# Head units by ScalarE a unit ahead, mix transfers on GpSimd's queue, an up tile moved before w_o, and a tail summed by TensorE, in a one-layer streaming encoder

## The chip, the cores and the metric

One core of one Trainium2 chip runs the whole program. The time is the device time of one execution in microseconds (us). The engines are TensorE (PE, matmuls), VectorE (DVE), ScalarE (ACT), GpSimd (POOL) and SyncE (SP, which here only issues DMA transfers). Each engine runs its own instructions in order and waits on semaphores for the others. A DMA is issued by an engine's instruction stream; here SP issues most, GpSimd and ScalarE a few.

## The reference, cut to what matters

1024 prompt frames and 32 sample frames of width 1024 go through one layer: an adaLN-modulated input gemm whose columns feed three head groups, one output gemm, a layer norm, a gated feed-forward part, and a second layer norm.

```python
h = x * (1 + sc1) + sh1
mq, mk, mv, mo, mi, mf, fq, fk, fv, ff, gu, gv = split(h @ w_in)
hm = head_norm(mlstm(mq, mk, mv, mi, mf)) * norm_g * sigmoid(mo)    # 4 heads of 64
hf = fox(fq, fk, fv, log_sigmoid(ff))                               # 8 heads of 64, causal softmax
hg = spatial_gate(gu, layer_norm(gv))                               # 4 groups of 64
mix = concat([hm, hf, hg]) @ w_o
x = layer_norm(ALPHA * x + (1 + g1) * mix)
h = x * (1 + sc2) + sh2
y = (silu(h @ w_gate) * (h @ w_up)) @ w_down
x = layer_norm(ALPHA * x + (1 + g2) * y)
```

Besides x, the keys and values of the heads, the mLSTM states and the gate inputs are outputs.

## The kernel before

**Arithmetic.** All data are fp32. Each operand of a large gemm is split into a part `hi` in a reduced format (float32r) and the rest `lo`, and a product is three matmuls, hi·hi, hi·lo and lo·hi (`gemm`, L117 to L119). Weights are loaded, `hi` is cast by ScalarE (L105) and `lo` is a subtraction on VectorE, or on GpSimd where a unit asks for that (L106). Activations are split in the same way (L922 and L923 for the mix that w_o reads). fp32 matmuls that are not split do transposes, the small products of the mixers, and the column sums of the layer norms (`ln_means`, L876, against a matrix of 1/1024).

**Layout.** Tokens lie in the free dimension, in two groups: group 0 has 512 prompt frames, group 1 the other 512 and the 32 sample frames. Features lie in 128-partition tiles. Intermediate head data (q, k as `dqh`, `dql`; mLSTM's `dmqk`, `dmv`, `dmo`; the gate input `dvn`; the mix `dmix`) go through DRAM: they are stored by one unit and loaded by another. `load` (L87) and `store` (L91) issue on SP's queue.

**Stages.** First adaLN and the gemm of the value units; then the gates; then a list ORDER of units: `q0` to `q7` are the gemms of q and k of one fox head (`fm_unit` with `evac_qk`), `k0`, `k1`, `o`, `v` the mLSTM projections, `s` its states, `f0` to `f7` the fox heads of group 0, `m0` to `m3` mLSTM tiles of 128 tokens, `a` pieces of the adaLN gemm. A `p` behind a unit gives its weight splits to GpSimd. Then come the gMLP gates (`evac_gv`, `evac_gmlp`, `to_mix`), w_o of group 0 with its norm, the remaining q units, and then the mixers of group 1 (fox heads in two parts, mLSTM tiles 4 to 8) woven into the up and down products of the feed-forward part of group 0. Before the last of these groups of up tiles (`g == WOB`) stands w_o of group 1, whose norm is woven into the up tiles left (`fill`). Then up, a variant of up with fewer products (`sup`), and down of group 1 follow, in two halves at the end, and the last layer norm (`ln2`).

**What sets the order.** The program is written as a sequence of units; a scheduler with a cost model then orders the instructions of each engine, with raised priority for the f and m units of ORDER, and with some instructions tied behind another (`issue_after`). Buffers are rings of a fixed count per name, so a new use of a name waits for the last reader of the buffer it gets.

**The places of the change.**
- `evac_qk` (L358 on) takes a finished q/k product out of PSUM: ScalarE writes `hi` (L366), VectorE writes `lo` from PSUM (L371), GpSimd adds them for `kr` (L372), and three stores follow.
- `mlstm` loads six pieces per tile: mqk, two for mqb, mv, mo, mb. ScalarE makes three passes over mo (L542 to L544), and GpSimd multiplies it by the norm's weight (L545).
- `to_mix` transposes a finished tile on TensorE, copies it out on ScalarE (L637, buffer `mixs`, of which there are two) and stores it to `dmix`. mLSTM calls it with k0 = 0, gMLP with k0 = 6.
- A fox head ends with a copy on ScalarE into `fo` (L762), an addition on VectorE into `fr` (L763) and a store to `dmix`. `foxbufs` are the buffer counts of a fox head's k1, qp, k2 and others; `fox_qp` is the name of the loaded queries (read by L706).
- `ln_sum` adds the z tiles of a layer norm on GpSimd and their squares on VectorE (L866), as each down tile is finished (L963). `ln_means` sums over the partitions. In `ln2` the mean is copied out (L1206), the variance is formed (L1207), each tile has its mean subtracted (L1209), is multiplied by 1/std (L1225), and gets its weight and bias from ScalarE (L1227) or, the last one, from VectorE (L1229).

Of the kernel before, what the change touches and what calls it, by code (L numbers as in the profile page):

```python
# [7 lines left out]
F32 = mybir.dt.float32  # L8
# [7 lines left out]
P = 128  # L16
D = 1024
KT = 8
# [23 lines left out]
ORDER = "q0 f0 q1 a f1 a q2 f2 k0 k1p s a q3 f3 a v q4 f4 a q5 f5 o a m0 q6 f6 a m1 a q7 m2 f7 a m3 a"  # L42
# [23 lines left out]
def f(ap):  # L66
    return ap.bitcast(F32)


class Kernel:  # L70
# [288 lines left out]
    def evac_qk(self, h, late=None):  # L359
# [3 lines left out]
        def evac(o, n, ps):  # L363
# [3 lines left out]
            if late:  # L367
                nc.scalar.activation(kr[:, :n], ps, AF.Copy, scale=self.qsc)
                nc.vector.tensor_tensor(lo[:, :n], kr[:, :n], f(hi[:, :n]), ALU.subtract)
            else:  # L370
                nc.vector.scalar_tensor_tensor(lo[:, :n], ps, self.qsc, f(hi[:, :n]), ALU.mult, ALU.subtract)  # L371
                nc.gpsimd.tensor_tensor(kr[:, :n], f(hi[:, :n]), f(lo[:, :n]), ALU.add)  # L372
# [146 lines left out]
    def mlstm(self, j):  # L519
# [7 lines left out]
        self.load(qk[:, :, :L], self.dmqk[:, :, o:o + L])  # L527
        qb = t([P, 2, 2, P], "mqb")
        nc.gpsimd.memset(qb, 0.0)
        for a in range(2):  # L530
            r = slice(64 * a, 64 * a + 64)
            self.load(qb[r, :, a, :L], self.dmqk[r, 0:2, o:o + L])
        v = t([P, 4, 65], "mv1", 1)
        nc.gpsimd.memset(v[:, :, 64:65], 1.0)
        self.load(v[:L, :, 0:64], self.dmv[:L, j, :].rearrange("p (h e) -> p h e", h=4))
        mo = t([P, 256], "mo", 1)
        self.load(mo[:L], self.dmo[:L, j, :])
        mb = t([P, 4, P], "mb", 1)
        self.load(mb[:L, :, :L], self.dM[:, j, :L].partition_broadcast(L))
# [90 lines left out]
    def to_mix(self, x, j, L, k0, pool, bank=None):  # L630
# [57 lines left out]
    def fox_chunk(self, h, tiles, W, nq, k1, k2, qp, q2, v):  # L688
# [151 lines left out]
    def ln_begin(self, eng, pivot=True, sum=True):  # L840
        t = lambda tag: self.t(self.pn, [P, 544], F32, tag, 2)
        return {"zs": t("zs"), "qs": t("qs"), "pv": t("pv"), "eng": eng, "pivot": pivot, "sum": sum,
                "order": range(KT), "late": (), "rest": []}
# [9 lines left out]
    def ln_sum(self, st, z, m, sl):  # L853
        nc = self.nc
        o = st["order"]
        if m == o[0]:
# [7 lines left out]
        st["eng"].tensor_tensor(st["zs"][:, sl], z[:, o[0], sl] if m == o[1] else st["zs"][:, sl],  # L864
                              z[:, m, sl], ALU.add)
        nc.vector.tensor_tensor(st["qs"][:, sl], st["qs"][:, sl], sq, ALU.add)  # L866

    def ln_means(self, st, sl):
# [3 lines left out]
        for i, x in enumerate(("zs", "qs")):  # L872
# [324 lines left out]
    def ln2(self, c, st, a, b, aff, late=False):  # L1197
# [8 lines left out]
        nc.scalar.copy(mean, pm)  # L1206
# [389 lines left out]
```

## Time and profile before

| | us |
|---|---|
| median of three runs | 1394.51 |
| the runs | 1390.44, 1394.51, 1396.62 |
| the profiled execution | 1393.61 |
| its span | 1391.1 |
| mean granted TensorE clock | 0.991 |
| DMA moved | 233.08 MB, mean 168 GB/s |

The span runs from the first to the last instruction of the profile; what lies around it makes the difference to the time of the execution. Sums below are made against the profiled execution. In the rows, a name `fm_g` is the stage (fm) and the tile (g); `out<-in` says what is written and read; L12 is line 12 of the kernel; `[2.46 <-DVE fm_qkl L371]` says that the engine stood idle for 2.46 us until that instruction of VectorE was done. A "q" behind an engine's name is its queue of DMA issues.

The busy shares of the engines over 40 equal slices, in tenths (9 is 90% or more):

```profile
PE   7999999999899999999999999999999999999996
DVE  5548646678679857777766767667997988888777
ACT  3323234444355744535454355435574554545355
POOL 0103200052156400000000000264610000000341
```

### The profile page before, as it was taken

What the parts mean: (1) busy time and instruction counts of PE and PEld (TensorE: products, weight loads), DVE (VectorE), ACT (ScalarE), POOL (GpSimd) and SP (SyncE); (2) the same over time, 40 slices, a digit from 0 to 9 for tenths busy, and PEclk for the clock granted to TensorE, in tenths of its full rate; (3) what the DMA queues carried; (4) which work ended last, traced back from release to release, by engine and by line L of the source; (5) the groups of instructions that cost most, each with busy time, mean ns of one, the idle gap of its engine ahead of it and who ended that gap; (6) DMA issues with size and microseconds to landing.
All of it is one profiled execution on the core that took longest, in us unless ns stands there. A gap on an engine that the chain in (4) does not pass through costs nothing.

```text
span 1391.1 us, 25980 instructions
## 1 busy us (share of the span) xinstructions
PE 1346.5 (97%) x9683; PEld 1240.3 (89%) x9683; DVE 1030.4 (74%) x2216; ACT 643.5 (46%) x1271; POOL 252.2 (18%) x280
## 2 busy tenths in 40 slices
PE   7999999999899999999999999999999999999996
PEld 4899988898799888888887889889999999999996
DVE  5548646678679857777766767667997988888777
ACT  3323234444355744535454355435574554545355
POOL 0103200052156400000000000264610000000341
PEclk9999999999999999999999999999999999999998
DMA  9754577587765754435435442555597767453321
GB/s 363 267 207 135 165 238 214 172 257 234 230 186 173 207 149 127 125 121 152 125 92 119 118 112 85 162 166 142 162 236 189 216 163 212 138 174 113 102 90 65
DMA packets 136372, 233.08 MB, mean 168 GB/s; under 512 B 22564, under 2 KB 79532, under 8 KB 136248
## 3 DMA queue, kind: packets, MB, share of 16 engines
q1 hardware_dynamic: 130936, 221.34, 51.0%
q0 software_dynamic: 5168, 9.96, 4.6%
q8 instruction: 76, 1.25, 0.4%
q14 instruction: 48, 0.39, 0.1%
q10 hardware_dynamic: 144, 0.14, 0.0%
HBM read 197.50 MB, written 53.81 MB: 181 GB/s over the span
## 4 chain that ended last, share of the span: by engine, by line
PE 69%; DVE 4%; DMA 3%; ACT 1%; issue 1%; SPq 0%; DVEq 0%; ACTq 0%
PE up_g L119 6%; PE up_g L118 5%; PE up_g L117 5%; PE dn_g L117 4%; PE dn_g L118 4%; PE dn_g L119 4%; PE sup_u L119 3%; PE sup_u L117 3%; PE sup_u L118 3%; PE wo_g L117 2%; PE wo_g L118 2%; PE wo_g L119 2%; PE sup_g L118 2%; PE sup_g L119 2%; PE sup_g L117 2%; PE fox_t L742 2%
## 5 line engine op out<-in xcount | busy, mean ns | idle before, releaser
L117 PE MATMUL up_g<-ada_ah,up_whi 128*128 128x512 f32 (+1 forms) x384 | 141.0, 367 | 1.9 <-DVE ada_adam L187 1.4
L118 PE MATMUL up_g<-ada_al,up_whi 128*128 128x512 f32 (+1 forms) x384 | 140.5, 366 | 0.0
L119 PE MATMUL up_g<-ada_ah,up_wlo 128*128 128x512 f32 (+1 forms) x384 | 139.5, 363 | 0.0
L117 PE MATMUL fm_g<-start_h1h,fm_whi 128*128 128x256 f32 (+2 forms) x344 | 102.8, 304 | 10.5 <-ACT tm_mixs L637 5.4
L284 PE MATMUL tm_g<-tm_whi,start_h1l 128*128 128x256 f32 (+1 forms) x384 | 109.9, 287 | 0.0
L282 PE MATMUL tm_g<-tm_whi,start_h1h 128*128 128x256 f32 (+1 forms) x384 | 109.7, 287 | 0.0
L283 PE MATMUL tm_g<-tm_wlo,start_h1h 128*128 128x256 f32 (+1 forms) x384 | 109.2, 285 | 0.0
L118 PE MATMUL fm_g<-start_h1l,fm_whi 128*128 128x256 f32 (+2 forms) x344 | 102.6, 298 | 0.2 <-DVE start_h1l L223 0.2
L119 PE MATMUL fm_g<-start_h1h,fm_wlo 128*128 128x256 f32 (+2 forms) x344 | 101.3, 296 | 0.0
L1125 ACT CAST sup_whi<-sup_raw 128x1024 fp32r<-128x1024 f32 x54 | 56.0, 1048 | 91.4 <-PE dn_u L118 47.9
L117 PEld LDWEIGHTS up_g<-ada_ah,up_whi 128*128 128x128 f32 x384 | 72.2, 188 | 13.7 <-DVE ada_adam L187 1.6
L105 ACT CAST up_whi<-up_raw 128x1024 fp32r<-128x1024 f32 x50 | 52.3, 1045 | 65.2 <-PE up_g L118 40.1
L118 PEld LDWEIGHTS up_g<-ada_al,up_whi 128*128 128x128 f32 x384 | 72.3, 188 | 11.2 <-issue 0.2
L119 PEld LDWEIGHTS up_g<-ada_ah,up_wlo 128*128 128x128 f32 x384 | 72.3, 188 | 11.0
L117 PEld LDWEIGHTS fm_g<-start_h1h,fm_whi 128*128 128x128 f32 x344 | 66.3, 194 | 16.2 <-ACT tm_mixs L637 5.7
L106 DVE TENSOR_TENSOR up_wlo<-up_raw,up_whi 128x1024 fp32r<-128x1024 f32 x50 | 63.1, 1261 | 19.0 <-ACT up_whi L105 18.6
L1126 DVE TENSOR_TENSOR sup_wlo<-sup_raw,sup_whi 128x1024 fp32r<-128x1024 f32 x54 | 68.0, 1263 | 10.8 <-ACT sup_whi L1125 10.8
L282 PEld LDWEIGHTS tm_g<-tm_whi,start_h1h 128*128 128x128 f32 x384 | 72.2, 189 | 2.8 <-issue 1.6
L117 PE MATMUL dn_g<-up_acth,dn_whi 128*128 128x512 f32 (+2 forms) x200 | 74.3, 373 | 0.0
L119 PE MATMUL dn_g<-up_acth,dn_wlo 128*128 128x512 f32 (+2 forms) x200 | 73.7, 368 | 0.0
L118 PE MATMUL dn_g<-up_actl,dn_whi 128*128 128x512 f32 (+2 forms) x200 | 73.6, 369 | 0.0
L284 PEld LDWEIGHTS tm_g<-tm_whi,start_h1l 128*128 128x128 f32 x384 | 72.2, 188 | 1.5 <-issue 1.2
(596 smaller groups left out, 4583.9 us busy)
## 6 DMA issues: line engine op xcount, KB each, us to landing
up_raw<-w_gu SPq DMA_DIRECT2D x50, 512.0 KB
ada_late<-w_ada SPq DMA_DIRECT2D x28, 512.0 KB
dn_raw<-w_dn SPq DMA_DIRECT2D x28, 512.0 KB
wo_raw<-w_o SPq DMA_DIRECT2D x24, 512.0 KB
ada_araw<-w_ada SPq DMA_DIRECT2D x20, 512.0 KB
sup_raw<-w_gu SPq DMA_DIRECT2D x20, 512.0 KB
start_dp<-w_gu SPq DMA_DIRECT2D x19, 512.0 KB
start_dp<-w_gu POOLq DMA_DIRECT2D x19, 512.0 KB, 7.8
```

Of the source, the lines that this page charges most:

```text
L105: nc.scalar.copy(hi[:, :w], raw[:, :w])
L106: (eng or nc.vector).tensor_tensor(lo[:, :w], raw[:, :w], f(hi[:, :w]), ALU.subtract)
L117: nc.tensor.matmul(ps, hi, xh(k), start=start and k == 0, stop=False)
L118: nc.tensor.matmul(ps, hi, xl(k), start=False, stop=False)
L119: nc.tensor.matmul(ps, lo, xh(k), start=False, stop=stop and k == n - 1)
L282: nc.tensor.matmul(ps[:, :ncol], xh, hi, start=k == 0, stop=False)
L283: nc.tensor.matmul(ps[:, :ncol], xh, lo, start=False, stop=False)
L284: nc.tensor.matmul(ps[:, :ncol], xl, hi, start=False, stop=k == 7)
L742: nc.tensor.transpose(ps[:, c:c + P], probs[y][:, b * P:(b + 1) * P], self.ident)
L1125: nc.scalar.copy(h, x)
L1126: tt(l, x, f(h), ALU.subtract)
```

## The change

1. `evac_qk`: `kr` is always written by ScalarE from PSUM, a second pass behind `hi`; `lo` is VectorE's subtraction of the two in SBUF. GpSimd's addition is gone.
2. ORDER: each q unit stands one unit further ahead of the fox head that reads it, `k1` has its weights split by VectorE, and fox_qp has two buffers for group 0.
3. The loads of the mLSTM tiles, the mix stores of mLSTM and fox, and the load of the gate input in `evac_gmlp` are issued by GpSimd instead of SP. gMLP's mix stores stay with SP. The fox result is written over `fo`; `fr` is gone.
4. At WOB, one more up tile of group 0 comes before w_o of group 1, and the fill behind it has one tile instead of two.
5. In the last half of the last layer norm (`onpe`), the z tiles are summed by TensorE, one matmul against the 1/1024 matrix for each, as they are finished; the mean is copied out with its sign turned; tiles 3 to 7 have the mean taken off in PSUM by two matmuls with the identity each; VectorE then multiplies from PSUM.

```diff
-ORDER = "q0 f0 q1 a f1 a q2 f2 k0 k1p s a q3 f3 a v q4 f4 a q5 f5 o a m0 q6 f6 a m1 a q7 m2 f7 a m3 a"
+ORDER = "q0 q1 f0 a q2 f1 a k0 f2 q3 k1 s a f3 q4 a v f4 q5 a o f5 q6 a m0 q7 f6 a m1 a f7 m2 a m3 a"
...
             nc.scalar.activation(hi[:, :n], ps, AF.Copy, scale=self.qsc)
-            if late:
-                nc.scalar.activation(kr[:, :n], ps, AF.Copy, scale=self.qsc)
-                nc.vector.tensor_tensor(lo[:, :n], kr[:, :n], f(hi[:, :n]), ALU.subtract)
-            else:
-                nc.vector.scalar_tensor_tensor(lo[:, :n], ps, self.qsc, f(hi[:, :n]), ALU.mult, ALU.subtract)
-                nc.gpsimd.tensor_tensor(kr[:, :n], f(hi[:, :n]), f(lo[:, :n]), ALU.add)
+            nc.scalar.activation(kr[:, :n], ps, AF.Copy, scale=self.qsc)
+            nc.vector.tensor_tensor(lo[:, :n], kr[:, :n], f(hi[:, :n]), ALU.subtract)
...
-        self.load(qk[:, :, :L], self.dmqk[:, :, o:o + L])
+        self.nc.gpsimd.dma_start(qk[:, :, :L], self.dmqk[:, :, o:o + L])
...
-        self.load(mo[:L], self.dmo[:L, j, :])
+        self.nc.gpsimd.dma_start(mo[:L], self.dmo[:L, j, :])
...
-        self.store(self.dmix[c][:, k0:k0 + 2, o:o + L], s[:, :, :L])
+        (nc.sync if k0 else nc.gpsimd).dma_start(self.dmix[c][:, k0:k0 + 2, o:o + L], s[:, :, :L])
...
-        self.load(vn[:n], self.dvn[:n, tt, :])
+        nc.gpsimd.dma_start(vn[:n], self.dvn[:n, tt, :])
...
-        r = t([64, nq], F32, "fr", 1)
         nc.scalar.copy(tmp[:, :nq], o[64:128, :nq])
+        r = tmp
         nc.vector.tensor_tensor(r[:, :nq], o[0:64, :nq], tmp[:, :nq], ALU.add)
...
-        self.store(self.dmix[c][64 * (h % 2):64 * (h % 2) + 64, 2 + h // 2, o:o + nq], r[:, :nq])
+        nc.gpsimd.dma_start(self.dmix[c][64 * (h % 2):64 * (h % 2) + 64, 2 + h // 2, o:o + nq], r[:, :nq])
...
+        if st["onpe"]:
+            if m == o[0]:
+                st["pm"] = self.t(self.pt, [P, 512], F32, "t")[:, :sl.stop - sl.start]
+            for x in st["wait"]:
+                nc.tensor.matmul(st["pm"], self.onesm, x, start=x is st["first"], stop=False)
+            st["wait"] = [z[:, m, sl]]
...
+        if onpe:
+            for k in range(3, KT):
+                p = centred[k] = self.t((self.pg, self.pu)[k % 2], [P, 512], F32, self.utag[k % 2])[:, :b - a]
+                nc.tensor.matmul(p, self.ident, z[:, k, sl], start=True, stop=False)
+                nc.tensor.matmul(p, self.ident, mean, start=False, stop=True)
...
-            elif k >= 3:
+            elif k >= 3 and not onpe:
                 with self.tc.issue_after(scaled.ins):
                     less(k)
-            scaled = nc.vector.tensor_tensor(zk, zk, r, ALU.mult)
+            scaled = nc.vector.tensor_tensor(zk, centred.get(k, zk), r, ALU.mult)
...
-        self.foxbufs = (2, 1, 1, 2, 3)
+        self.foxbufs = (2, 2, 1, 2, 3)
...
                 weave(self.up(0, j0 + 1, act, pa, MM[0]))
+                weave(self.up(0, j0 + 2, act, pa, MM[0]))
...
-                    for j in range(j0 + 2, j0 + nj):
+                    for j in range(j0 + 3, j0 + nj):
...
             if half:
                 st["late"] = st["order"][6:]
+                st["onpe"] = True
```

Three places show how instructions move. The first is SP's queue where the gMLP gates end and w_o of group 0 begins; `start_dmix_33` and `start_dmix_32` are the mix of the two groups in DRAM, `ada_z` the residual input, `wo_tmp` the mix as w_o loads it. Before:

```order
L91 DMA start_dmix_32_88<-mlstm_mixs_4316 128x2x128
L87 DMA ada_z_843_4352<-xT 128x512 x8
L87 DMA wo_tmp_4363<-start_dmix_32_88 128x256
L87 DMA wo_tmp_4367<-start_dmix_32_88 128x256
L87 DMA wo_tmp_4371<-start_dmix_32_88 128x256
L87 DMA wo_tmp_4375<-start_dmix_32_88 128x256
L91 DMA start_dmix_33_89<-tm_mixs_5032 128x2x128
L91 DMA start_dmix_33_89<-tm_mixs_5074 128x2x128
```

In the changed kernel:

```order
L91 DMA o_vn<-tm_traw_4967 32x256
L636 DMA start_dmix_33_89<-tm_mixs_5024 128x2x128
L636 DMA start_dmix_33_89<-tm_mixs_5066 128x2x128
L87 DMA ada_z_835_4344<-xT 128x512 x8
L87 DMA wo_tmp_4355<-start_dmix_32_88 128x256
L87 DMA wo_tmp_4359<-start_dmix_32_88 128x256
L87 DMA wo_tmp_4363<-start_dmix_32_88 128x256
L87 DMA wo_tmp_4367<-start_dmix_32_88 128x256
L636 DMA start_dmix_33_89<-tm_mixs_5108 128x2x128
```

The two gMLP mix stores have moved from behind the eight loads of z and four of wo_tmp to ahead of them. The loads of wo_tmp for the last two mix blocks (not in these rows) now stand behind the stores of the last head unit.

The second is the load of mo for the last mLSTM tile (32 tokens). Before, on SP:

```order
L91 DMA o_n<-fm_C_2472 128x1x1
L87 DMA dn_raw_10081<-w_dn 128x1024
L87 DMA mlstm_mo_7875<-start_dmo_62 32x256
L87 DMA fox_v_7838<-start_dv_59 128x8x128
L91 DMA start_dmix_33_89<-fox_fr_7824 64x256
```

In the changed kernel, on GpSimd:

```order
L528 DMA mlstm_mqb_7850<-start_dmqk_60 64x2x32 x2
L762 DMA start_dmix_33_89<-fox_fo_7668 64x256
L523 DMA mlstm_mqk_7848<-start_dmqk_60 128x4x32
L530 MEMSET mlstm_mv_1530_7854 128x4
L531 DMA mlstm_mv_1530_7854<-start_dmv_61 32x4x64
L533 DMA mlstm_mo_7857<-start_dmo_62 32x256
L762 DMA start_dmix_33_89<-fox_fo_7806 64x256
L541 TENSOR_TENSOR mlstm_mo_7857<-mlstm_mo_7857,start_rowp_176 32x256
```

The load no longer stands between weight loads, and now shares an in-order queue with fox stores and with GpSimd's multiplication of mo (L541 there).

The third is the end of TensorE's program, behind the last down product (`lnb_t` and `dn_t` are sums, `lnb_g` and `lnb_u` the centred tiles). Before:

```order
L119 MATMUL dn_u_16790<-up_acth_16587,up_al_2883_16413 128x272
L876 MATMUL lnb_t_16810<-sup_zs_15778,start_onesm_138 128x272
L876 MATMUL lnb_t_16810<-wo_z_2067_10819,start_onesm_138 128x272
L876 MATMUL lnb_t_16814<-sup_qs_15779,start_onesm_138 128x272
L876 MATMUL lnb_t_16814<-dn_tmp_16784,start_onesm_138 128x272
L876 MATMUL lnb_t_16810<-wo_z_2067_10819,start_onesm_138 128x272
L876 MATMUL lnb_t_16814<-dn_tmp_16804,start_onesm_138 128x272
```

In the changed kernel:

```order
L119 MATMUL dn_u_16768<-up_acth_16563,up_al_2859_16389 128x272
L886 MATMUL lnb_t_16790<-sup_qs_15755,start_onesm_138 128x272
L1231 MATMUL lnb_g_16809<-wo_z_2056_10924,start_ident_121 128x272
L1231 MATMUL lnb_g_16815<-wo_z_2056_10924,start_ident_121 128x272
L857 MATMUL dn_t_16637<-wo_z_2056_10924,start_onesm_138 128x272
L886 MATMUL lnb_t_16790<-dn_tmp_16762,start_onesm_138 128x272
L880 MATMUL dn_t_16637<-wo_z_2056_10924,start_onesm_138 128x272
L1231 MATMUL lnb_u_16806<-wo_z_2056_10924,start_ident_121 128x272
L1231 MATMUL lnb_u_16812<-wo_z_2056_10924,start_ident_121 128x272
L1231 MATMUL lnb_u_16818<-wo_z_2056_10924,start_ident_121 128x272
L886 MATMUL lnb_t_16790<-dn_tmp_16783,start_onesm_138 128x272
L1232 MATMUL lnb_u_16806<-sup_zs_15754,start_ident_121 128x272
```

Up to the last sum of squares ten matmuls stand where six stood, and the matmuls with the mean follow.

More of the change, by code (lines that the diff above doesn't have):

```diff
@@ L842, in ln_begin @@
         return {"zs": t("zs"), "qs": t("qs"), "pv": t("pv"), "eng": eng, "pivot": pivot, "sum": sum,
-                "order": range(KT), "late": (), "rest": []}
+                "order": range(KT), "late": (), "rest": [], "onpe": False, "wait": [], "first": None}
     def ln_pivot(self, st, z, sl):
@@ L855, in ln_sum @@
         o = st["order"]
+        if st["onpe"]:
[4 more added lines that the diff above has]
+            st["wait"] = [z[:, m, sl]]
+            if m == o[0]:
+                st["first"] = st["wait"][0]
         if m == o[0]:
@@ L871, in ln_means @@
         out = []
-        for i, x in enumerate(("zs", "qs")):
+        if st["onpe"]:
+            for n, x in enumerate(st["wait"]):
+                self.nc.tensor.matmul(st["pm"], self.onesm, x, start=False, stop=n == len(st["wait"]) - 1)
+            out.append(st["pm"])
+        for i, x in list(enumerate(("zs", "qs")))[len(out):]:
             p = self.t(self.pt, [P, 512], F32, "t")[:, :sl.stop - sl.start]
```

17 lines of the change are left out of this document (10 added, 7 removed).

## The prediction

> **What bounds the kernel now.** I read the busy shares first, then the list of waits of TensorE (PE), then stretches around its stalls.
>
> ```profile
> PE 1346.5 (97%) x9683; PEld 1240.3 (89%) x9683; DVE 1030.4 (74%) x2216; ACT 643.5 (46%) x1271; POOL 252.2 (18%) x280
> ...
> PE fm_g L117 <- ACT tm_mixs L637: 5.4, 2, 4.7
> PE wo_g L117 <- ACT up_ah L922: 3.3, 2, 3.0
> PE fox_s L706 <- DMA fox_qp<-start_dql: 3.3, 2, 2.4
> PE fm_g L117 <- DVE fm_qkl L371: 2.5, 1, 2.5
> PE fox_t L742 <- ACT mlstm_mixs L637: 2.0, 1, 2.0
> ...
> PE fox_s L706 <- issue: 1.4, 1, 1.4
> ```
>
> TensorE is busy in 1346.5 of 1391.1 us, so all of its idle time is 44.6 us and nothing but that, and what idling does to the clock, can be won. The matmul work stays the same but for the tail. The six rows, all in places that the diff touches, sum to 17.9 us. Idle time costs twice when the clock falls after it:
>
> ```profile
> core 0: us, PE busy (x) PEld busy (x) DVE busy (x) ACT busy (x) POOL busy (x), PEclk, DMA share, GB/s
> 140.60:144.10 3.50, 3.46 (x16) 3.46 (x17) 3.35 (x6) 2.01 (x4) 2.46 (x4) 0.51 0.41 129
> 144.10:147.60 3.50, 3.50 (x31) 3.50 (x31) 3.40 (x6) 0.38 (x1) 3.38 (x5) 1.00 0.33 57
> 203.10:206.50 3.40, 3.39 (x29) 3.40 (x30) 2.03 (x6) 1.59 (x4) 0.00 (x0) 1.00 0.36 121
> 376.20:383.00 6.80, 5.75 (x26) 5.64 (x26) 0.78 (x3) 1.23 (x5) 0.00 (x0) 0.50 0.81 259
> 765.30:768.70 3.40, 3.40 (x10) 2.62 (x9) 1.93 (x6) 1.99 (x6) 0.00 (x0) 0.50 0.70 193
> 908.60:912.10 3.50, 3.45 (x16) 3.13 (x15) 1.66 (x4) 1.59 (x4) 0.00 (x0) 0.51 0.31 86
> ```
>
> At a granted clock of 0.51, 16 matmuls fit where 31 fit in the next stretch of the same length: half of such a stretch is lost, 1.7 us each at 140, 765 and 908, and 3.4 us at 376. These four stretches follow the stalls of 2.5, 2.0, 3.0 and 4.7 us. The longest wait of fox_s for fox_qp, 2.4 us, ends at 203.1 and has a clock of 1.00 behind it, so a stall of this size may or may not cost its own length again. I charge each of the four.
> The Trainium skill ("TensorE: Matmul & The Clock Gate", "HAM oscillation — how this bites in real kernels") makes it a rule that idle gaps of over about 3.4 us bring the half rate back. By it only the 4.7 us at 377 would be charged, the other three slow stretches would stay, and the sum below would be 5.1 us poorer, about 1384. The trace differs: 0.50 and 0.51 stand behind stalls of 2.0, 2.5 and 3.0 us.
>
> **Head units (L366 to L372, ORDER).** Five rows of the timeline before the stall that ends at 140.64, and the matmul that ends it; the number in brackets is the idle time.
>
> ```profile
> 136.25 2.46 DVE L444 TENSOR_SCALAR gates_fr<-gates_fr 8x256 fp32r<-8x256 f32 x1
> 140.11 0.48 DVE L371 SCALAR_TENSOR_TENSOR fm_qkl<-fm_g,start_qsc,fm_qkh 128x272 fp32r<-128x272 f32 x1
> 140.62 0.29 DVE L444 TENSOR_SCALAR gates_fr<-gates_fr 8x256 fp32r<-8x256 f32 x1
> 135.49 0.46 ACT L366 ACTIVATE fm_qkh<-fm_g,start_qsc 128x256 fp32r<-128x256 f32 x1
> 136.14 2.43 POOL L106 TENSOR_TENSOR fm_wlo<-fm_raw,fm_whi 128x1024 fp32r<-128x1024 f32 x1
> 140.64 0.58 PE L117 MATMUL fm_g<-start_h1h,fm_whi 128*128 128x256 f32 x1 [2.46 <-DVE fm_qkl L371]
> ```
>
> One operation of VectorE took 2.46 us instead of 0.29, just while GpSimd's split of unit k1's weights ran; L371, which reads PSUM, came late behind it, and TensorE waited for the bank. Both leave: the split goes to VectorE, and the bank is now read only by ScalarE, twice (L366, 0.46 us, and a second pass of the same form). VectorE's subtraction then reads SBUF and holds no bank. ScalarE is at 46%, and its second read follows the first in its queue, so what could delay it already delayed the first. Gain 2.5 + 1.7 = **4.2 us** (bounds 0, if another bank wait comes, and 4.2).
> The waits of fox_s for fox_qp and for issue, 3.3 + 1.4 = 4.7 us, come from a head's q and k being stored to DRAM and loaded back right before its use; with the q unit one unit ahead, and a second fox_qp buffer, the round trip lies behind a whole head. Gain **4.7** (bounds 2.4 and 4.7).
>
> **gMLP's mix stores and loads.** What SP issued, and ScalarE and TensorE behind it:
>
> ```profile
> 365.68 3.76 SPq L87 DMA_DIRECT2D ada_z<-xT  x8
> 369.48 2.69 SPq L87 DMA_DIRECT2D wo_tmp<-start_dmix  x4
> 372.54 0.37 SPq L91 DMA_DIRECT2D start_dmix<-tm_mixs  x1
> 376.82 0.37 ACT L637 COPY tm_mixs<-tm_g 128x256 f32<-128x256 f32 x1 [0.17 <-DMA start_dmix<-tm_mixs]
> 377.25 0.59 PE L117 MATMUL fm_g<-start_h1h,fm_whi 128*128 128x272 f32 x1 [4.70 <-ACT tm_mixs L637]
> ```
>
> The first mix store of the gate tiles stood on SP behind eight loads of z and four of wo_tmp; the third copy into the two mixs buffers had to wait until it landed, and held PSUM. In the changed order the two stores stand ahead of both groups. Gain: waits 4.7 + 0.7 (the rest of the 5.4) and 3.4 of clock = 8.8. It gives something back: the loads of wo_tmp for the last two mix blocks now stand on SP behind five stores of the last head unit, and w_o of group 0 begins with them. SP issued four wo_tmp in 2.69 us; I take 2.5 as late (bounds 0 and 6). Net **-6.3**.
>
> **mLSTM's loads and the mix stores on GpSimd's queue.** The loads of mo (durations in ns), the stall at 764, and the transfers that GpSimd issues already:
>
> ```profile
> L87 SPq DMA_DIRECT2D mlstm_mo<-start_dmo x9: 319/332/2865, 251.6 to 752.5; - x9
> 752.50 2.87 SPq L87 DMA_DIRECT2D mlstm_mo<-start_dmo  x1
> 761.52 0.42 ACT L542 ACTIVATE mlstm_mo<-mlstm_mo 32x256 f32<-32x256 f32 x1 [6.49 <-DMA mlstm_mo<-start_dmo]
> 764.66 0.33 PE L742 MATMUL fox_t<-start_ident,fox_p 128*128 128x128 f32 x1 [1.99 <-ACT mlstm_mixs L637]
> L1077 POOL DMA_DIRECT2D start_dp<-w_gu x19: 1026/1035/1507, 931.2 to 1229.8; - x19
> DMA to landing us min/median/max: 6.1/7.8/12.2
> ```
>
> At 752 the last tile's mo was issued late, ScalarE stood 6.49 us before L542 with L637 behind it, and TensorE lost 2.0 + 1.7 = 3.7 us. The move takes 9 x 6 loads, 9 + 24 mix stores and 9 gate loads, 96 transfers, from SP to GpSimd. SP loses 0.33 us of issue for most; GpSimd gains 96 x 1.035 = 99 us by the nearest row, on an engine that is busy 252 us of 1391. So its capacity is no bound; its order is. It runs in order: behind a waiting mo load or L545 (which waits for ScalarE's three passes over mo) stand the store of a fox head and the loads of the next tile. A fox store that is late holds the one buffer "fo" now that "fr" is gone, then PSUM bank fox_o, then TensorE's next head. A store needs 1 + 7.8 us by the rows, and the next head's scores, exponentials, transposes and products come before it copies into "fo", so mostly this stays covered. I take the gain of 3.7 as **-3.0**, and for new waits of this queue **+5.5**: one and a half of the nine tiles paying what the one at 752 paid (bounds 0 and nine times, 33). One in nine was late on SP, and GpSimd's queue is shorter but dearer in each entry, hence a little more than one.
>
> **One up tile more ahead of w_o of group 1.** From the chain of waits, and the matmul behind it:
>
> ```profile
> 903.71 5.58 DMA wo_tmp<-start_dmix
> 907.80 0.39 PE L117 MATMUL wo_g<-up_ah,wo_whi 128*128 128x272 f32 x1 [3.04 <-ACT up_ah L922]
> ```
>
> w_o waits for the last mix block to be stored, loaded and split. The tile's 96 matmuls, at the 31 in 3.5 us of the stretch from 144.1, are 10.8 us of work, far above the 3.3 us of the waits, so it goes with its 1.7 of clock: 5.0. The same tile is missing later, under the norm of group 1, where one tile of fill is left instead of two. VectorE does most of that norm's steps, and TensorE would run dry if the norm's first half came late. The first half's statistics, though, follow w_o at once, ahead of the tile that is left, so I take 0.5 as given back (bounds 0 and 5). Net **-4.5**.
>
> **Tail.** The last sums on TensorE, then the first and last steps behind them on VectorE and ScalarE:
>
> ```profile
> 1375.87 0.73 PE L876 MATMUL lnb_t<-sup_zs,start_onesm 128*128 128x272 f32 x2 [0.15 <-POOL sup_zs L864]
> 1378.49 0.62 PE L876 MATMUL lnb_t<-wo_z,start_onesm 128*128 128x272 f32 x2
> 1378.95 0.62 PE L876 MATMUL lnb_t<-dn_tmp,start_onesm 128*128 128x272 f32 x2
> 1379.68 0.50 DVE L1207 SCALAR_TENSOR_TENSOR lnb_tmp<-lnb_t,start_epsa,lnb_tmp 128x272 f32<-128x272 f32 x1 [1.85 <-ACT lnb_tmp L1205]
> 1382.57 1.15 DVE L1225 TENSOR_TENSOR wo_z<-wo_z,sup_pv 128x272 f32<-128x272 f32 x3
> 1387.89 0.42 DVE L1229 TENSOR_SCALAR wo_z<-wo_z,start_colp 128x272 f32<-128x272 f32 x1
> 1383.05 2.14 ACT L1227 ACTIVATE wo_z<-wo_z,start_colp 128x272 f32<-128x272 f32 x4 [1.94 <-DVE wo_z L1225]
> ```
>
> A fp32 matmul of 272 columns costs 1378.95 - 1378.49 = 0.46 us. Six of the new column sums lie inside the last down product, where TensorE is never idle: +2.7 us. Behind the last product ten fp32 matmuls stand up to the last sum of squares (4.6 us) where six stood before (from 1375.87 - 0.15 = 1375.7 to 1378.95 + 0.62 = 1379.6, with their waits 3.9 us): +0.7. So the statistics are ready 3.4 us later. From the first multiply VectorE took 1387.89 + 0.42 - 1382.57 = 5.7 us, alternating subtractions and multiplies; now it only multiplies, and ScalarE's seven passes at 2.14 / 4 = 0.535 set the pace, 0.44 + 7 x 0.535 = 4.2: -1.5. Net **+1.9** (bounds +0.5, if a sum in the down product costs only one of its two passes, and +3.5, if the multiplies from PSUM are no faster).
>
> **The sum.** -4.2 - 4.7 - 6.3 - 3.0 + 5.5 - 4.5 + 1.9 = -15.3 us against the profiled execution's 1393.6, that is 1378.3. The median of the runs is 0.9 above that execution, so I forecast **1379 us**. With all gains and no new wait it is -4.2 - 4.7 - 8.8 - 3.7 - 5.0 + 0.5 = -25.9; about 1368 is the low end. The likeliest case alone spans 1369 to 1389.
>
> **Rivals.**
> Everything works and GpSimd's queue costs nothing: without the +5.5 it is 1373. For it speaks GpSimd's 18%, against it that one mo in nine was late even on SP.
> The stalls only move: the gMLP term keeps 2.8 (6 given back), the extra tile nothing (5 given back under the norm), the heads 2.4, mo 1.0, the tail costs 3.5; k1 stays. -4.2 - 2.4 - 2.8 - 1.0 + 3.5 + 5.5 = -1.4, about 1393, no change. For it speaks that VectorE has little left where it takes over k1's split: 3.35 of 3.50 us busy in the stretch from 140.6.
> Slower: the in-order GpSimd queue delays mo or the next tile's mqk in every tile, 9 x 3.7 = 33 us against the other gains of 17.8: +15.5, about 1410. It decides if GpSimd reaches the loads of a tile less than ten us (1 + 7.8 and an issue) ahead of ScalarE's L542. For it speaks that L545, which has ScalarE's three passes ahead of it, now holds fox stores and the next tile's loads behind it; against it that a tile's own loads all stand ahead of its L545 in the new order.
> Slower still: VectorE starves GpSimd's transfers. L444 was held 2.2 us by GpSimd; if every transfer ahead of mo were held so, six of them make mo 13 us late, 4 more than the lead, and each tile costs 2.0 + 4 + 1.7: 69 - 17.8, about 1446. Against it stands that 19 such transfers, beside a VectorE at 74%, took 1.507 us at most. The Trainium skill ("SBUF — State Buffer", the box on the DVE blocks DMA trap) says that GpSimd cannot write descriptors during VectorE's two-port operations. The row of L1077 shows at most 0.5 us of it.
>
> **How the numbers follow.** The likeliest case 0.55, all gains 0.14, moved stalls 0.19, the slower queue 0.09, starvation 0.03. A measurement of this kernel cannot tell less than 0.5%, 7 us: faster is below 1387.5, slower above 1401.5. Faster: most of 0.55 (0.51), 0.14 and a tenth of 0.19: 0.67. Slower: 0.12. No change: 0.21. The range 1368 to 1396 leaves out the two slower cases and a little at each end.
>
> **What would show it.** Right: the wait rows of fm_g for L637 and L371, of wo_g for the ah cast and of fox_s for fox_qp are gone, the granted clock stays at 1.00 from 60 us to the end, and TensorE's idle time falls from 44.6 to about 30 us. The tail after the last product grows by about 2 us. Wrong: fox_t or mlstm_s waiting for rows fed by GpSimd's loads, new half-clock stretches between 400 and 950, or stalls of up_g between 955 and 1010.

## The result, and the profile after

| | before | changed |
|---|---|---|
| median of the runs | 1394.75 us (6 runs) | 1413.33 us (6 runs) |
| span of the profiled execution | 1391.1 us | 1414.4 us |
| mean granted TensorE clock | 0.991 | 0.987 |

The changed kernel is slower: ratio 1.0134, 95% interval 1.0117 to 1.0150, that is 18.6 us, where 16 us less than before were forecast. Each set of runs below has its own runs of the kernel before. Ratios are against those, and what a run wins against the changed kernel is taken as the difference of the two ratios. The profiled execution of the changed kernel was the slowest of its six (1416.19 us), so the traces differ by 23.3 us of span where the medians differ by 18.6.

TensorE's share on the page, and its longest waits (waited for: us in total, times, longest):

```profile
PE 1360.2 (96%) x9713; PEld 1251.4 (88%) x9713; DVE 1026.6 (73%) x2212; ACT 652.0 (46%) x1295; POOL 283.7 (20%) x346
...
PE wo_g L117 <- ACT ada_ah L932: 6.2, 1, 6.2
PE tm_g L649 <- ACT tm_traw L644: 4.2, 2, 2.2
PE ada_t L179 <- DMA ada_late<-w_ada: 3.6, 2, 3.1
PE mlstm_s L568 <- issue: 2.3, 1, 2.3
PE fox_s L702 <- ACT fox_p L711: 2.1, 1, 2.1
PE fox_s L703 <- DMA fox_k<-start_dql: 2.0, 1, 2.0
...
PE fox_t L738 <- ACT mlstm_mixs L633: 1.8, 1, 1.8
```

The waits of fm_g for L371, of fox_s for fox_qp by way of its own DMA, and of w_o of group 1 are gone from the list. In their place stand waits of w_o of group 0, of the gate products (L649, before L653), and of loads for the adaLN weights (ada_late) and the fox heads. All idle time is now 1414.4 - 1360.2 = 54.2 us instead of 44.6; the other 13.7 us of the 23.3 are busy time, in which lie 30 more matmuls and more half clock. Stretches by window:

```profile
core 0: us, PE busy (x) PEld busy (x) DVE busy (x) ACT busy (x) POOL busy (x), PEclk, DMA share, GB/s
173.10:179.90 6.80, 6.22 (x32) 5.09 (x31) 0.91 (x4) 0.37 (x1) 0.00 (x0) 0.50 0.68 165
207.30:210.70 3.40, 3.40 (x16) 3.40 (x17) 2.06 (x8) 1.19 (x5) 0.00 (x0) 0.51 0.41 134
330.10:333.50 3.40, 3.40 (x18) 3.40 (x17) 3.29 (x15) 0.54 (x2) 1.92 (x4) 0.50 0.52 124
377.90:384.70 6.80, 6.55 (x31) 6.55 (x32) 0.86 (x4) 0.75 (x3) 0.54 (x1) 0.50 0.14 40
415.50:422.30 6.80, 3.91 (x18) 3.91 (x18) 1.96 (x5) 2.16 (x5) 0.00 (x0) 0.50 0.40 142
```

Half of TensorE's busy time in these five is 11.7 us, against 8.5 charged for four before. A sixth stretch, from 538.0 to 541.4 with a granted clock of 0.55, has no wait of TensorE in the 38 us ahead of it. Half clock between 400 and 950 was one of the prediction's signs of being wrong.

Where the 23.3 us of span were lost, from the same stage in both traces ("first" is a start, "last" an end; the order is new, so the tile is not always the same one):

| event on TensorE | before | changed | later by |
|---|---|---|---|
| last transposition of the gates | 163.60 | 160.72 | -2.9 |
| last transposition of a gMLP tile (tm_g) | 385.16 | 398.74 | 13.6 |
| first sum of group 0's norm (lna_t) | 441.68 | 463.02 | 21.3 |
| last fox product (fox_o) | 886.37 | 907.74 | 21.4 |
| first down product of dn_u, after w_o of group 1 | 980.79 | 995.51 | 14.7 |
| first sup product, after group 1's norm | 1037.72 | 1058.12 | 20.4 |
| last up product (up_u) | 1363.61 | 1384.39 | 20.8 |
| end of the span | 1391.1 | 1414.4 | 23.3 |

The loss lies between the gates and the norm of group 0: in the ORDER loop, at the gMLP gates and at w_o. SP's issues there in the changed kernel (start, duration, issue):

```profile
378.40 8.84 SPq L636 DMA_DIRECT2D start_dmix<-tm_mixs  x2
387.54 5.81 SPq L87 DMA_DIRECT2D ada_z<-xT  x8
393.59 1.77 SPq L87 DMA_DIRECT2D wo_tmp<-start_dmix  x4
```

The two gMLP mix stores stand ahead of the loads, as the listing showed. But their data were not there: SP stood at them from 378.40 to 387.24, and z and wo_tmp, issued at 365.68 and 369.48 before, came at 387.54 and 393.59. The second store had to wait for ScalarE's copy of a tile that TensorE transposed only at 385.99, at the end of the half clock from 377.9:

```profile
386.47 0.37 ACT L633 COPY tm_mixs<-tm_g 128x256 f32<-128x256 f32 x1
```

TensorE pays:

```profile
418.39 1.01 PE L117 MATMUL wo_g<-ada_ah,wo_whi 128*128 128x256 f32 x3 [6.20 <-ACT ada_ah L932]
```

Why the gates were late is seen on GpSimd's timeline of the changed kernel:

```profile
353.82 0.59 POOL L642 DMA_DIRECT2D tm_gvn<-start_dvn  x1 [4.88 <-DMA start_dvn<-tm_traw]
354.41 0.76 POOL L523 DMA_DIRECT2D mlstm_mqk<-start_dmqk  x1
355.18 0.76 POOL L353 TENSOR_TENSOR tm_traw<-tm_traw,start_rowp 128x256 f32<-128x256 f32 x1
356.02 0.81 POOL L354 TENSOR_TENSOR tm_traw<-tm_traw,start_rowp 128x256 f32<-128x256 f32 x1
...
370.94 0.80 POOL L354 TENSOR_TENSOR tm_traw<-tm_traw,start_rowp 32x256 f32<-32x256 f32 x1
```

A gate load (L642) waits until the store of the same gate tile has landed in DRAM. On GpSimd it waits in the queue that also has to multiply the next gate tiles by the norm's weights (L353, L354), and these feed the next stores. So the queue stands 4.88 us at a load while the multiplications behind it are late. The last of the nine ends at 371.74; in the kernel before:

```profile
360.54 0.73 POOL L354 TENSOR_TENSOR tm_traw<-tm_traw,start_rowp 32x256 f32<-32x256 f32 x1
```

That is 361.27, 10.5 us earlier. Not all of this comes from the loads. The first of the nine was late already. Its rows before and changed:

```profile
295.60 0.73 POOL L353 TENSOR_TENSOR tm_traw<-tm_traw,start_rowp 128x256 f32<-128x256 f32 x1 [1.24 <-DVE tm_traw L352]
301.44 0.74 POOL L353 TENSOR_TENSOR tm_traw<-tm_traw,start_rowp 128x256 f32<-128x256 f32 x1 [2.80 <-DVE tm_traw L352]
```

So 5.8 of the 10.5 us were lost further up, with the waits and half clocks near 172 and 207, and a part of that is this one execution: in the trace of a_mixact below, where GpSimd and TensorE have the same order up to there, the first came at 296.88. From the start of the first to the end of the last it is 65.7 us before and 70.3 changed. Over all traces of this document it is 68.8 to 72.4 us in the seven with the gate loads on GpSimd, and 62.1 to 68.4 in the thirteen with them on SP. That, some 4 to 5 us, is what the loads do to this queue.

### The profile page after: what moved, and what is told of

It reads as the page before. It is cut to its first block, busy times and chain, and to the rows that moved or that the text cites. A ratio compares the mean times of both kernels' runs of the same rounds, so it can differ in the third digit from the quotient of the medians.

```text
span 1414.4 us, 26078 instructions
## 1 busy us (share of the span) xinstructions
PE 1360.2 (96%) x9713; PEld 1251.4 (88%) x9713; DVE 1026.6 (73%) x2212; ACT 652.0 (46%) x1295; POOL 283.7 (20%) x346
## 4 chain that ended last, share of the span: by engine, by line
PE 80%; DMA 8%; DVE 5%; issue 4%; ACT 2%; SPq 1%; POOL 0%; ACTq 0%; DVEq 0%; POOLq 0%
PE up_g L117 5%; PE up_g L119 5%; PE up_g L118 5%; PE dn_g L117 4%; PE dn_g L119 4%; PE dn_g L118 4%; PE fm_g L117 3%; PE fm_g L118 3%; PE sup_u L118 3%; PE fm_g L119 3%; PE sup_u L119 3%; PE sup_u L117 2%; PE tm_g L283 2%; PE tm_g L282 2%; PE tm_g L284 2%
## 5 line engine op out<-in xcount | busy, mean ns | idle before, releaser
L117 PE MATMUL fm_g<-start_h1h,fm_whi 128*128 128x272 f32 (+2 forms) x344 | 101.8, 301 | 4.7 <-ACT fm_whi L105 1.9
L118 PE MATMUL fm_g<-start_h1l,fm_whi 128*128 128x272 f32 (+2 forms) x344 | 102.0, 296 | 0.0
L119 PE MATMUL fm_g<-start_h1h,fm_wlo 128*128 128x272 f32 (+2 forms) x344 | 100.8, 294 | 0.0
L117 PEld LDWEIGHTS up_g<-ada_ah,up_whi 128*128 128x128 f32 x384 | 72.7, 189 | 13.6 <-DVE ada_adam L187 1.6
L283 PEld LDWEIGHTS tm_g<-tm_wlo,start_h1h 128*128 128x128 f32 x384 | 74.3, 194 | 2.1 <-issue 1.2
L1136 DVE TENSOR_TENSOR sup_wlo<-sup_raw,sup_whi 128x1024 fp32r<-128x1024 f32 x54 | 68.0, 1264 | 10.1 <-ACT sup_whi L1135 9.9
L711 ACT ACTIVATE fox_p<-fox_s,fox_fmx 128x384 f32<-128x384 f32 (+2 forms) x96 | 55.1, 578 | 41.9 <-DVE fox_fmx L709 27.4
```

The costliest lines, as they stand in the source:

```text
L117: nc.tensor.matmul(ps, hi, xh(k), start=start and k == 0, stop=False)
L118: nc.tensor.matmul(ps, hi, xl(k), start=False, stop=False)
L119: nc.tensor.matmul(ps, lo, xh(k), start=False, stop=stop and k == n - 1)
L283: nc.tensor.matmul(ps[:, :ncol], xh, lo, start=False, stop=False)
L711: nc.scalar.activation(pr[:, lo:hi], banks[x][:, :hi - lo], AF.Exp, bias=mxs[:, 0:1], accum_out=sums[:, x:x + 1])
L1136: tt(l, x, f(h), ALU.subtract)
```

## The experiments: each part alone

The first runs put one part each into the kernel before. The diffs are those of the change.

**p_queue**, part 3: 

> The kernel before with part 3 alone (mLSTM loads, mLSTM and fox mix stores and the gate loads issued by GpSimd). Theory Q (the new order of the transfers makes the loss): 8 to 20 us slower than before, with the two long waits of SP for the gMLP mix copies ahead of the loads of z and wo_tmp, and w_o of group 0 waiting 4 us or more. Theory H (the head units a unit ahead make the loss): within 5 us of before.

1403.82 us, ratio 1.0052 (1.0032 to 1.0072): 7.3 us slower, just under what Q expected, above H. SP's order has one of the two mix stores ahead of z here, not both, and w_o of group 0 waits only 0.6 and 0.5 us. In this trace the gate products wait 2.0 us at 324, and the stall at the last mLSTM tile is longer, not gone: 3.2 us at 768.

**p_head**, parts 1 and 2: 

> The kernel before with parts 1 and 2 alone (kr by ScalarE, the new ORDER with k1 split by VectorE, two fox_qp buffers, the fox result written over fo, which makes room for the second buffer). Theory Q: 4 to 9 us faster than before, as forecast. Theory H: 5 to 14 us slower, with TensorE waiting for ada_late or fox_k near 170 to 210 us.

1399.86, ratio 1.0022 (0.9998 to 1.0046): no gain, as H, but less of a loss than H said. The gates end 4.5 us earlier than before (159.05), so the stall at 138 is cured. Behind them the gain is used up by nine waits of 0.7 to 1.8 us between 166 and 309, for ada_late, fox_k and fox_p among others, and by 4.3 us at 365 for the gate products.

**p_up**, part 4: 

> The kernel before with part 4 alone (one more up tile ahead of w_o of group 1). The forecast said 4.5 us faster; the trace of the changed kernel says 6.6 us gained at w_o and 5.7 given back under the norm, so 1 us faster, within 2 of before.

1394.96, ratio 0.9971 (0.9945 to 0.9997): 4.0 us faster. Against the trace of before it is 1.6 us late at the first up product, 5.2 us early at the first dn_u product behind w_o of group 1 (6.8 won), and 0.9 early at the end of the up products (4.3 given back under the norm).

**p_tail**, part 5: 

> The kernel before with part 5 alone (sums and centring by TensorE in the last half of the last norm). By the forecast 1.9 us slower, by the trace of the changed kernel 2.5 us slower; a rival says that both hide something else and it is within 1 us.

1400.94, ratio 1.0025 (1.0007 to 1.0043): 3.5 us slower, by the interval 1 to 6.

The four add up to 9.9 us; the whole costs 18.6.

## The experiments: one cause at a time

**e_gate.** `evac_qk` as in the change, and of ORDER only this:

```diff
-ORDER = "q0 f0 q1 a f1 a q2 f2 k0 k1p s a
+ORDER = "q0 f0 q1 a f1 a q2 f2 k0 k1 s a
```

> The kernel before with kr by ScalarE and k1 split by VectorE, without the new ORDER. If the first stall (near 140 us) is cured by these two edits and the loss of the head units comes from the order, this is 3 to 6 us faster than before. If the edits themselves cost elsewhere, it is within 2 us, or slower.

1396.49, ratio 1.0006 (0.9990 to 1.0021). The gates end at 158.95 instead of 163.60, and the whole gains nothing: the second expectation. Its trace waits 2.1 us for fox_k at 167 and 2.4 us for a gate load at 381, both with a half clock behind them, and 1.3 us for fm_qkr at 389. By this trace the stall removed early was worth nothing by the time that the gMLP gates were reached.

**e_mo2.** This edit, and the fox result over `fo` as in the change, which makes room for it:

```diff
-        mo = t([P, 256], "mo", 1)
+        mo = t([P, 256], "mo", 2)
```

> The kernel before with two buffers for mo (room for it by writing the fox result over fo) and nothing else. The theory that the late mo load waited for its one buffer, read by VectorE's product of the tile before (it was issued at 752.50, 0.03 us after that read ended), says the stall near 764 us and the half clock behind it go: 2 to 6 us faster. The theory of the prediction, that SP's queue held it, says the stall stays: within 1.5 us.

1390.08, ratio 0.9945 (0.9925 to 0.9965): 7.7 us faster, more than expected; the fox result over `fo` was not run alone, so the 7.7 us are those of both. The buffer, not the queue, made mo late. In the kernel before the timeline of VectorE says it, beside SP's issue at 752.50 that the prediction shows:

```profile
752.06 0.41 DVE L625 TENSOR_TENSOR mlstm_mhm<-mlstm_mhm,mlstm_mo 128x256 f32<-128x256 f32 x1
```

In the changed kernel the load stands on GpSimd and waits for the same read (L621 there):

```profile
775.88 0.52 POOL L533 DMA_DIRECT2D mlstm_mo<-start_dmo  x1 [6.80 <-DVE mlstm_mhm L621]
```

With two buffers all nine loads are issued by 694.9, and neither the stall near 764 nor the half clock behind it is there; what waits for mo's DMA, summed, was 16.4 us before and is now:

```profile
  DMA mlstm_mo<-start_dmo: 7.0, 6
```

**a_mixact.** In the changed kernel:

```diff
-        (nc.sync if k0 else nc.gpsimd).dma_start(
+        (nc.scalar if k0 else nc.gpsimd).dma_start(
```

> The changed kernel with gMLP's mix stores issued by ScalarE instead of SP. If SP, standing 8.84 us at two such stores ahead of the loads of z and wo_tmp, makes w_o of group 0 wait, the stalls at 412 to 428 us go and it is 6 to 11 us faster than the changed kernel, about 1404. If w_o is late for what lies upstream (gate loads, order), it stays within 3 us of 1413.

1409.19, ratio 1.0087 (1.0063 to 1.0111): by the ratios 6.6 us of the 18.6 (2.5 to 10.6 by the intervals), the low end of the first expectation; by the times themselves 4 us, between the two. The loads of z are no longer behind stores, but took SP from 368.36 to 384.30 all the same, and wo_tmp came at 384.54:

```profile
368.36 15.94 SPq L87 DMA_DIRECT2D ada_z<-xT  x8
384.54 2.51 SPq L87 DMA_DIRECT2D wo_tmp<-start_dmix  x4
```

The profile puts 10.1 us of SP's waits in this stretch to the landing of two of these same stores, now issued by ScalarE, so this run does not free the loads of them. The place of the stores is a part of the loss; the rest is not shown by this run.

**a_sp.** The changed kernel with the transfers of part 3 back on SP. 

> The changed kernel with all of part 3's transfers back on SP (the fox result still over fo). If the parts simply add, their single results give 1397.1 + 3.1 - 4.0 + 3.5, about 1400. If what is beyond the sum (18.6 measured, 9.9 from the parts) comes from the order of the units alone, it stays above 1406.

1400.34, ratio 1.0021 (1.0002 to 1.0040), on the number that the parts' sum gives. By the ratios the queue part costs 15.8 us in company, 7.3 alone.

**p_gvn** and **p_mload**, the kernel before with one kind of transfer moved, this line in the first and the five lines of `mlstm` in the second:

```diff
-        self.load(vn[:n], self.dvn[:n, tt, :])
+        nc.gpsimd.dma_start(vn[:n], self.dvn[:n, tt, :])
```

> The kernel before with only the gate loads of gMLP on GpSimd's queue (9 transfers). If they are what costs in the queue part (7 us alone), 4 to 8 us slower; if the mLSTM loads or the stores are, within 3 us.

1397.97, ratio 1.0021 (0.9997 to 1.0044): about 3 us, not resolved from none. Yet its multiplications end almost as late as in the changed kernel:

```profile
369.75 0.73 POOL L354 TENSOR_TENSOR tm_traw<-tm_traw,start_rowp 32x256 f32<-32x256 f32 x1
```

That is 370.48, 9.2 us later than before. But SP has z's loads ahead of the gMLP stores here, and issued them at 376.12 instead of 387.54. In the kernel before, late multiplications alone do not make the loss.

> The kernel before with only the 54 loads of the mLSTM tiles on GpSimd's queue. If GpSimd's own work and waits delay them, 4 to 8 us slower, with tiles m2 and m3 later than before; if the stores or the gate loads carry the cost, within 3 us.

1391.56, ratio 0.9985 (0.9966 to 1.0004): alone, the mLSTM loads cost nothing.

Then one kind was taken back in the whole change.

**a_gvnsp.**

```diff
-        nc.gpsimd.dma_start(vn[:n], self.dvn[:n, tt, :])
+        self.load(vn[:n], self.dvn[:n, tt, :])
```

> The changed kernel with the gate loads of gMLP back on SP. If they, on a queue that also multiplies by the norm's weight for the same gate tiles, cost most of the 13 us that the queue part costs in company, 7 to 12 us faster than the changed kernel; if the 3 us that they cost alone is all, 2 to 4.

1395.83, ratio 1.0006 (0.9990 to 1.0023). Nine loads moved back to SP take away all of the loss that can be measured, 17.8 us by the ratios, more than the 12 expected at most. The last multiplication for the gates, on GpSimd's timeline of this kernel:

```profile
363.30 0.81 POOL L354 TENSOR_TENSOR tm_traw<-tm_traw,start_rowp 32x256 f32<-32x256 f32 x1
```

and SP's issues:

```profile
371.61 0.37 SPq L636 DMA_DIRECT2D start_dmix<-tm_mixs  x1
372.27 3.73 SPq L87 DMA_DIRECT2D ada_z<-xT  x8
376.16 2.56 SPq L87 DMA_DIRECT2D wo_tmp<-start_dmix  x4
```

The multiplications end 7.6 us earlier than in the changed kernel (2.7 earlier than in a_mixact), wo_tmp is loaded 17.4 us earlier, no wait of w_o is over 0.6 us, and the norm of group 0 begins at 444.37 instead of 463.02. One store stands ahead of z instead of two: the scheduler orders SP anew with the loads there, and TensorE from 321 us on, so this kernel differs in that too. That the place of the nine loads, with the order that follows from it, makes the loss is shown; through which of the two queues is not.

**a_storesp.**

```diff
-        (nc.sync if k0 else nc.gpsimd).dma_start(self.dmix[c][:, k0:k0 + 2, o:o + L], s[:, :, :L])
+        self.store(self.dmix[c][:, k0:k0 + 2, o:o + L], s[:, :, :L])
...
-        nc.gpsimd.dma_start(self.dmix[c][64 * (h % 2):64 * (h % 2) + 64, 2 + h // 2, o:o + nq], r[:, :nq])
+        self.store(self.dmix[c][64 * (h % 2):64 * (h % 2) + 64, 2 + h // 2, o:o + nq], r[:, :nq])
```

> The changed kernel with the mLSTM and fox mix stores back on SP. If the stores on GpSimd's queue carry the cost (alone the loads of mLSTM cost nothing), 7 to 12 us faster than the changed kernel; if the gate loads do, within 4 us of it.

1405.11, ratio 1.0076 (1.0051 to 1.0101), 8 us faster than the changed kernel, as the first expectation has it.

**a_loadsp**, the five lines of `mlstm`, as

```diff
-        self.nc.gpsimd.dma_start(qk[:, :, :L], self.dmqk[:, :, o:o + L])
+        self.load(qk[:, :, :L], self.dmqk[:, :, o:o + L])
```

> The changed kernel with the 54 mLSTM loads back on SP. Alone these loads cost nothing when moved (0.9985), so within 4 us of the changed kernel; if in company they are what delays tiles m2 and m3, and with them z and w_o, 7 to 12 us faster.

1401.52, ratio 1.0064 (1.0041 to 1.0086), 9.8 us faster (1.0134 - 1.0064 = 0.0070 of 1394), though alone they cost nothing.

**a_noorder**, the two lines ORDER and `foxbufs`:

```diff
-        self.foxbufs = (2, 2, 1, 2, 3)
+        self.foxbufs = (2, 1, 1, 2, 3)
```

> The changed kernel with the old ORDER (k1's weights split by GpSimd again, one fox_qp buffer), all else as changed. If the 8.7 us beyond the sum of the parts lie between the new order and the new queue, it falls by more than the order's own cost: 8 to 12 us faster than the changed kernel, near 1403. If not, it stays within 4 us of 1413.

1406.76, ratio 1.0081 (1.0053 to 1.0110), 7 us faster, between the expectations.

Taking back any one of the four helps by 7 to 18 us, 43 together out of 18.6. So these are not separate costs. Three of the four stand on GpSimd's queue, the new ORDER does not; where they meet is read from the traces. The ratio follows the issue of the first wo_tmp loads: 376.16 in a_gvnsp (1.0006), 379.79 in a_sp (1.0021), 383.54 in a_loadsp (1.0064), 384.54 in a_mixact (1.0087), 385.62 in a_noorder (1.0081), 385.95 in a_storesp (1.0076) and 393.59 in the changed kernel (1.0134). The gate loads are the ones without which nothing measurable is left.

**c_up_mo2**, the kernel before with part 4 and mo's second buffer: 

> The kernel before with one more up tile ahead of w_o of group 1 and two buffers for mo (fox result over fo). If the two gains are independent, 7.7 + 4.0 = 11.7 us faster than before, 9 to 14. If the second only shifts the wait to another place, 6 to 8.

1388.75, ratio 0.9974 (0.9963 to 0.9985), against 0.9945 for the buffer alone: the gains do not add. In the trace of e_mo2, w_o of group 1 waited 1.3 and 0.9 us and no half clock followed, so little was left for the tile to save, and under the norm it gave back as before.

**c_up_mo2_act**, that with gMLP's mix stores on ScalarE: 

> c_up_mo2 with gMLP's mix stores issued by ScalarE. If the stall near 377 us (4.7 us and 3.4 us of half clock) comes from the stores' place on SP behind the loads of z and wo_tmp, it goes without giving w_o a new wait: 4 to 9 us faster than c_up_mo2. If the gate loads or the tile m3 are late as well, within 2 us of it.

1391.01, ratio 0.9992 (0.9978 to 1.0007): not faster. Of the 4.7 us at the mixs buffer 1.4 and 0.9 are left; the gate products wait 1.6 and 1.0 us, and w_o of group 0 1.3. In the trace of c_up_mo2 the wait at 377 was already another: 4.0 us for a gate load.

**c_new**, the changed kernel with gate loads on SP as in a_gvnsp, and

```diff
-        mo = t([P, 256], "mo", 1)
+        mo = t([P, 256], "mo", 2)
...
-        self.foxbufs = (2, 2, 1, 2, 3)
+        self.foxbufs = (2, 1, 1, 2, 3)
...
-                st["onpe"] = True
```

> The changed kernel with the gate loads back on SP, the tail as before, two buffers for mo and one for fox_qp. If the single results add (1.0006, tail -0.25%, mo -0.55%), 0.9926 of before, some 10 us faster; if mo's gain is partly what the up tile already saves (as in c_up_mo2), 0.995 to 0.997.

1390.79, ratio 0.9974 (0.9959 to 0.9989), just above the range of the second expectation.

**c_old**, c_new with the old ORDER: 

> c_new with the old ORDER (k1's weights split by GpSimd). If the new order still costs its 3 us, this is 2 to 5 us faster than c_new; if the order was only bad together with the gate loads, within 2 us or slower, since the stall near 140 us is back.

1391.63, ratio 0.9985 (0.9972 to 0.9998). The two orders cannot be told apart once the gate loads are off GpSimd's queue. The lowest ratio of all runs is that of e_mo2, one buffer more and nothing of the change but the fox result over fo.

## Why the prediction was wrong, point by point

**What bounds the kernel: right.** TensorE's idle time and its clock decide, and what was lost shows there, but for the matmuls that the tail adds.

**Head units: the first stall right, the gain not kept.** The term of 4.2 us was there at the gates (4.5 in p_head, 4.7 in e_gate). But the term was read as a gain of the whole, and e_gate shows that it is not (1.0006). The 4.7 us for the q units a unit ahead failed: parts 1 and 2 together are no gain (1.0022). The step that failed is "the round trip lies behind a whole head". fox_qp's wait left the list, and waits for fox_k and for the loads of the adaLN weights took its place; they go through the same queue of SP. That this queue is the reason is argued, not shown.

**gMLP's stores, -6.3: wrong sign; the step that failed most.** It took the place of an instruction in the queue for the time at which it runs. The stores do stand ahead of the loads, but whoever stands in an in-order queue ahead of its data holds all behind it: 8.84 us at two stores. The bound of 6 us for what wo_tmp could give back was too small (6.2 + 0.7 + 1.3 us of stalls, and 6.8 us at half clock of which TensorE was busy in 3.9). And it did not ask when the gate tiles would be ready, which part 3 changes. By a_gvnsp the loss goes with the gate loads; by p_gvn they cost some 3 us where SP's stores do not stand ahead of z. The stall of 4.7 us was also not the stores' alone: c_up_mo2_act moves them off SP and wins nothing.

**mLSTM's loads, -3.0: the mechanism was wrong.** SP's issue at 752.50 was read as the queue's lateness; it was the end of VectorE's last read of the one buffer, 0.03 us before. The 1.75 us stall is still there after the change, and a second buffer removes it.

**New waits of GpSimd's queue, +5.5: the size too small, the place wrong.** Alone, part 3 was priced -6.3 - 3.0 + 5.5 = -3.8 and measured +7.3, in company +15.8. The price was set by mo; the queue in fact held the gate tiles' multiplications, by some 4 to 5 us from the first to the last. The rival with a slower queue gave 1410 and the chance 0.09, with the right engine and kind of mechanism, but through mo and mqk in every tile, and that is not what happened: the loss is at one stage. That its 1410 lies close to 1413 is luck. Starvation by VectorE did not show: the nine gate loads took 0.527 to 0.612 us to issue and landed in 2.3 to 5.5, and none of the 87 other transfers that moved took as much as 1 us to issue.

**The up tile, -4.5: right in size for another sum.** 4.0 alone. 6.8 were won at w_o, and 4.3 given back under the norm, where 0.5 was taken from bounds of 0 and 5. The waits under the norm in the changed kernel:

```profile
1023.15 0.39 PE L118 MATMUL up_g<-wo_al,up_whi 128*128 128x272 f32 x1 [1.04 <-DVE wo_al L1016]
...
1033.17 0.39 PE L117 MATMUL up_g<-wo_ah,up_whi 128*128 128x272 f32 x1 [1.68 <-ACT wo_ah L1015]
1039.05 0.39 PE L117 MATMUL up_u<-wo_ah,up_whi 128*128 128x272 f32 x1 [0.97 <-ACT up_whi L105]
```

**Tail, +1.9: right step by step, 0.7 us missing.** From the end of TensorE, VectorE and ScalarE in the changed kernel:

```profile
1403.91 0.50 DVE L1218 SCALAR_TENSOR_TENSOR lnb_tmp<-lnb_t,start_epsa,lnb_tmp 128x272 f32<-128x272 f32 x1 [4.15 <-PE lnb_t L886]
...
1406.80 1.15 DVE L1242 TENSOR_TENSOR wo_z<-wo_z,sup_pv 128x272 f32<-128x272 f32 x3
```

```profile
1407.27 3.64 ACT L1244 ACTIVATE wo_z<-wo_z,start_colp 128x272 f32<-128x272 f32 x7 [1.94 <-DVE wo_z L1242]
1410.94 0.37 ACTq L1249 DMA_DIRECT2D o_yT<-wo_z  x1
```

The down product ends 2.7 us later against the last up product (1399.21 - 1384.39 against 1375.72 - 1363.61), as forecast. The variance follows it after 4.7 us instead of 4.0: +0.7, as forecast. From the first multiply to the last step it is 4.1 us (to ScalarE's last pass) instead of 5.7 (to VectorE's): -1.6, as forecast (-1.5). But the span ends 3.5 us after that last step, instead of 2.8: why the last store takes longer from ScalarE's queue is not seen. Sum +2.5; alone 3.5 by the runs.

**The range** ended 17 us under the result, with the slower cases outside it. The sum added gains read from single stalls, each as if the rest stayed in place.

## What stays open

Why e_gate loses its gain again, and why the tile and the buffer do not add, is read from single profiles only. The mix stores of mLSTM and fox were never moved alone in the kernel before, and neither was the fox result over fo. How the loss divides between GpSimd's late multiplications and SP's stand at the stores is not settled: p_gvn has the first without the second and loses some 3 us. The second without the first is in c_new, where SP was at two gMLP stores from 370.64 for 5.38 us ahead of z; it has 0.9974, where the single results add up to 0.9926, but it differs in the buffers and the tail as well.

## What to carry to other kernels

Before a load is moved to another engine's queue, ask what it waits for: a load that waits for a store to land must not stand ahead of work that feeds the next store. A late DMA issue is not yet a late queue: look what ended within 0.1 us before it, often the last read of the buffer, and then a second buffer may be the cure. A transfer early in an in-order queue is early only if its data are; and a stall that is removed is a gain only if the next meeting point of the engines comes earlier too.

## What the runs showed of the hardware

The half clock is not a property of the program. In p_tail every engine has the order of the kernel before up to the last half, yet its profiled execution was 8.2 us later at the last up product: its half clock also came at 204 behind a stall of 2.75 us, and stayed 6.8 instead of 3.4 us at 771 behind one of 3.55. In the changed kernel stalls of 2.0 us (205) and 2.2 us (327) had one behind them, and ones of 2.1 us (258) and 2.3 us (315) had none; that at 538 had no stall ahead of it. So a difference of some us between two single profiles is not yet an effect. The Trainium skill ("TensorE: Matmul & The Clock Gate", "HAM oscillation — how this bites in real kernels") draws the line at idle gaps of about 3.4 us; here 2.0 us were enough, and 2.1 us not always.

A small operation of VectorE was held while GpSimd worked, in another place than before: one column took 3.31 us, usually 0.2. GpSimd's 128x1024 subtraction ran from 313.22 for 2.39 us and its 128x256 addition from 315.56 for 0.72; VectorE's operation ended 0.03 us after that. TensorE waited 2.3 us behind it, for a tile that VectorE wrote next.

```profile
313.00 3.31 DVE L339 SCALAR_TENSOR_TENSOR tm_brt<-tm_bmv,start_eps,tm_brs 128x1 f32<-128x1 f32 x1
```
